# Wide matmuls in the first feed-forward product of a two-block transformer kernel

## The chip, the cores and the metric

The kernel runs on one core of one Trainium2 chip. The metric is the time of one execution on the device, in microseconds (us). Engines are named as in the profile: PE (TensorE, with its weight loads as PEld), DVE (VectorE), ACT (ScalarE), POOL (GpSimd) and SP, whose queue issues the loads of the weights.

## What is computed

Two transformer blocks over 256 tokens of width 1024, in float32. The first ends with a feed-forward part, and this is the part that the change touches:

```python
hf = rmsnorm(x, norm_ff_g[l])
z = jax.nn.relu(jnp.einsum('bsd,df->bsf', hf, w_ff1[l]))
x = x + jnp.einsum('bsf,fd->bsd', z * z, w_ff2[l])
```

Its inner width is 4096, which the kernel cuts into eight blocks of 512 columns. The second block (gated linear attention, block attention, 32 experts) follows, and its expert weights, 3 x 32 matrices of 2 MB, are the largest part of what is read.

## The kernel before

**Numbers in two parts.** Each float32 operand of a product is split into an upper part, rounded to the format fp32r, and a lower part, the remainder. A product is three matmuls: upper weights times upper activation, upper weights times lower activation, lower weights times upper activation. The weights are split on the fly: `conv` (L197 to L218) lets ACT copy a piece of 128 x 1024 into `whi` (L215), and then DVE or POOL subtracts to get `wlo` (L216). I call the ACT instruction the cast of a unit and the subtraction its split.

**Units.** Work goes in units: one unit is one such piece, half a loaded slot of 1 MB, and 24 matmuls of 256 columns. `unit_mm` (L220) records its matmuls, all in L246 for this part of the program. There are four buffers for each of `whi` and `wlo` (`NB = 4`), so the cast of unit j + 4 can only run when unit j has been multiplied, and it has the three units between them as its time. The main loop records, for unit j: the matmuls, then what evacuates a finished product, then `conv(j + 4)`, and then, while there are any, one operation of `adaq`. Splits of units with j % 4 = 1, and here also j % 8 = 4, go to POOL, three of eight; the other five go to DVE.

**The `adaq` operations** (L357) are 128 x 1024 multiply-and-sum operations on DVE that compute the second block's modulation from weights (w_adaT) loaded meanwhile. Behind every fourth there is a tiny addition (L362). 24 of them fall into the feed-forward part. They have no hurry of their own, but DVE's instructions stand in one queue, in the order written.

**The feed-forward part.** First product, block c: `f1(c)`, four units. Second product, block c: `f2(c)`, four units. The order is f1(0), f1(1), f2(0), f1(2), f2(1), f1(3), f2(2), ..., f1(7), f2(6), f2(7), which are units 80 to 143: f1(c) for c from 2 on is units 76 + 8c to 79 + 8c, f2(c) is units 88 + 8c to 91 + 8c. The result of f1(c) is used eight units later, so it is in no hurry.

**Evacuation of f1(c)** (`ev_f1`, L545 to L557), behind the last of its four units: for each of two PSUM banks, DVE takes relu and multiplies by the norm factor (L552, reading PSUM and one SBUF tile), ACT squares (L555), and `split` makes the two parts of z, the upper by ACT (L262), the lower by DVE (L264). Only then comes `conv` of unit j + 4.

Of the kernel before, what the change touches and what calls it, by code (L numbers as in the profile page):

```python
# [26 lines left out]
OV = 12  # L27

# [43 lines left out]
def tile_fused(ctx: ExitStack, tc: tile.TileContext, I, out):  # L72
# [146 lines left out]

    def unit_mm(j, units):  # L220
        g, kp = units[j]
        if g.mode == "G":
            mm_gates(convd.pop(j))
            return
        if g.mode == "L":
            if kp:
                mm_last(g, (convd.pop(j - 1), convd.pop(j)))
            return
        whi, wlo = convd.pop(j)
        ahi, alo = g.act()  # L230
        if kp == 0 and g.first:
            g.ps = [bank(b) for b in g.banks]
        if kp == 0 and not g.first:
            g.ps = g.prev.ps
        for kk in range(2):
            k = 2 * kp + kk
            ka = g.k0 + k
            lastk = g.last and k == g.nk - 1
            firstk = g.first and k == 0
            if g.mode == "F":  # L240
                for m in range(4):
                    o = g.ps[m // 2][:, (m % 2) * 256:(m % 2 + 1) * 256]
                    c = slice(m * 128, (m + 1) * 128)
                    pairs = ((whi, ahi), (whi, alo), (wlo, ahi))
                    for i, (w, a) in enumerate(pairs):
                        pe.matmul(o, w[:, kk, c], a[:, ka, :], start=firstk and i == 0 and m % 2 == 0,  # L246
                                  stop=lastk and i == 2, skip_group_check=True)
            else:
                for n in range(2):
                    o = g.ps[n]  # L250
                    c = slice(n * 128, (n + 1) * 128)
                    pairs = ((ahi, whi), (ahi, wlo), (alo, whi))
                    for i, (a, w) in enumerate(pairs):
                        pe.matmul(o, a[:, ka, c], w[:, kk, :], start=firstk and i == 0,
                                  stop=lastk and i == 2, skip_group_check=True)
        if kp == g.nk // 2 - 1 and g.last and g.evac:
            g.evac(g.ps)
# [8 lines left out]
    def half_of(name, m, t):  # L266

        return A[name][0][:, m:m + 2, :], A[name][1][:, m:m + 2, :], t
# [59 lines left out]
    A = {}  # L328
    st = {}

    def pair(tag, name):
        A[name] = tuple(big(f"{tag}{i}", (128, 8, 256), F32R) for i in range(2))
# [177 lines left out]
    def ev_wo(ch):  # L510
        def f(ps):
            if ch == 0:
                pair("E", "xg")
            for j in range(2):
                m = 4 * ch + 2 * j
                x1 = xT[:, m:m + 2, :]
                dve.tensor_tensor(x1, v2(ps[j]), x1, op=OP.add)
                for i in (m, m + 1):
                    act.activation(A["xg"][0][:, i, :], xT[:, i, :], AF.Copy, scale=V("gff", i))
            for i in range(4 * ch, 4 * ch + 4):  # L520
                dve.scalar_tensor_tensor(A["xg"][1][:, i, :], xT[:, i, :], V("gff", i),
                                         A["xg"][0][:, i, :].bitcast(F32), op0=OP.mult, op1=OP.subtract)
# [21 lines left out]
    def ev_f1(c):  # L544
        def f(ps):  # L545
            if c == 0:
                st["z"] = [big(f"H{i}", (128, 2, 4, 256), F32R) for i in range(2)]
            t4 = st["z"][c % 2]
            A["z", c] = (t4[:, 0], t4[:, 1])
# [6 lines left out]
            split(*(half_of(("z", c), 2 * j, t) for j, t in enumerate(ts)))  # L556
        return f  # L557
# [58 lines left out]
    def bn_hn():  # L616
# [34 lines left out]
    def mm_gates(w):  # L651
        ps = bank(7)
        for k in range(8):
            for i in range(2):
                pe.matmul(ps[:, 0:256], w[:, k, :], A["hn"][i][:, k, :], start=k == 0 and i == 0,
                          stop=k == 7 and i == 1)
# [109 lines left out]
    def mix_in(i, tag):  # L766
        t = big(tag, (128, 2, 4, 256), F32R)
        A["mix", i] = (t[:, 0], t[:, 1])
# [158 lines left out]
    def at_o(m, b):  # L927
# [12 lines left out]
        split((A["mix", 1][0][:, m, :], A["mix", 1][1][:, m, :], ps[:, 0:256]))  # L940
# [27 lines left out]
    def mm_last(g, w):  # L968

        ahi, alo = g.act()  # L970
        for m in (0, 2, 1, 3):
            o = g.prev.ps[m // 2][:, (m % 2) * 256:(m % 2 + 1) * 256]
            c = slice(m * 128, (m + 1) * 128)
            for k in range(4):
                whi, wlo = w[k // 2]
                for i, (x, a) in enumerate(((whi, ahi), (whi, alo), (wlo, ahi))):
                    pe.matmul(o, x[:, k % 2, c], a[:, k, :], start=False, stop=k == 3 and i == 2, skip_group_check=True)
# [193 lines left out]
    def f1(c, hooks=None):  # L1171
        add_group(next_slot(I["w_ff1"][c], 2), "F", "xg", ev_f1(c), hooks)
# [148 lines left out]
    def x_g(k):  # L1321
        hi, lo = A["xg"][0][:, k, :], A["xg"][1][:, k, :]
# [25 lines left out]
    def x_h(k0):  # L1348
        for k in range(k0, k0 + 2, 2):
            t = tmp()  # L1350
            pool.tensor_tensor(t, xT[:, k:k + 2, :], st["rxb"][:, None, :].to_broadcast([128, 2, 256]), op=OP.mult)
            for i in range(2):
                hi = A["h"][0][:, k + i, :]
                act.activation(hi, t[:, i, :], AF.Copy, scale=V("gmix", k + i))
                dve.scalar_tensor_tensor(A["h"][1][:, k + i, :], t[:, i, :], V("gmix", k + i), hi.bitcast(F32),
# [4 lines left out]
    for s in steps:  # L1360
        if s[0] == "u":
# [342 lines left out]
def layout(inputs):  # L1704
# [15 lines left out]

    a = {"x": f["x"], "xT": np.ascontiguousarray(f["x"][0].T.reshape(8, 128, 256).transpose(1, 0, 2))}
    a["w_in"] = kpc(f["w_in"][0]).reshape(7, 2, 2, 128, 2048)
    for n in ("w_proj_a", "w_proj_b", "w_out"):
        a[n] = kpc(f[n][0])
    a["w_ff1"] = kpc(f["w_ff1"][0])
# [60 lines left out]
```

## Time and profile before

| what | value |
|---|---|
| three runs, median (lowest to highest) | 1041.33 us (1040.93 to 1042.59) |
| the profiled execution's own time | 1041.49 us |
| its span, first to last instruction | 1039.8 us |
| PE busy, share of the span | 1003.6 us, 97% |
| DVE / ACT / POOL busy | 515.0 / 354.1 / 216.8 us |
| read from HBM | 325.13 MB |

Times in the trace count from the start of the span. The feed-forward part lies between about 244 and 431 us, the experts between about 600 and 1040 us. A group of instructions merged in a row has a start, a length, a count (x3) and, in brackets, the idle time of the engine just before it and what ended it. "PE busy" counts overlapping matmuls once and says little of how densely they are packed; their start times do.

### The profile page before, as it was taken

The page shows a single profiled execution, that of the slowest core. Times are in us where ns is not written, and L with a number is a line of the kernel's source. Part 1 is how long each engine was busy: PE and PEld are TensorE (multiplying, and loading weights), DVE is VectorE, ACT ScalarE, POOL GpSimd, SP SyncE. Part 2 cuts the span into 40 slices and gives each one's busy share as a digit, 9 for nine tenths or more (in the row PEclk, how much of TensorE's full clock was granted, in tenths as well). Part 3 has the DMA queues.
Part 4 walks back from the last instruction along what each step waited for, and adds up shares of the span by engine and source line. Part 5 has one row for each costly group of instructions (what it writes and reads, how often), then busy time and mean ns, then how long its engine had stood idle before and what let it go on. Part 6 is the DMA issues. An engine that isn't in the chain of part 4 may idle for free. (4 is left out here: it accounts for less than half of the span.)

```text
span 1039.8 us, 16067 instructions
## 1 busy us (share of the span) xinstructions
PE 1003.6 (97%) x6690; PEld 738.0 (71%) x6690; DVE 515.0 (50%) x767; ACT 354.1 (34%) x528; POOL 216.8 (21%) x137
## 2 busy tenths in 40 slices
PE   9999999999999999989999999999999998888996
PEld 6999999999999999878989634343434343433443
DVE  5787985477589863489784422121212121111112
ACT  6554543454543454455465311010101010100111
POOL 1333422235343334166343200000000000000100
PEclk9999999999999999999999999999999999999999
DMA  8964787665578965435649699999999999998995
GB/s 335 417 261 163 279 329 285 207 239 180 185 289 298 343 248 200 162 130 195 232 144 370 234 418 419 422 421 421 421 422 421 420 421 422 420 418 343 420 419 216
DMA packets 51796, 327.27 MB, mean 315 GB/s; under 512 B 5896, under 2 KB 8712, under 8 KB 15112
## 3 DMA queue, kind: packets, MB, share of 16 engines
q1 hardware_dynamic: 51432, 325.68, 80.4%
q8 instruction: 54, 0.88, 0.3%
q10 hardware_dynamic: 288, 0.52, 0.1%
q14 instruction: 22, 0.18, 0.0%
HBM read 325.13 MB, written 1.05 MB: 314 GB/s over the span
## 5 line engine op out<-in xcount | busy, mean ns | idle before, releaser
L215 ACT ACTIVATE whi<-w 128x1024 fp32r<-128x1024 f32 x178 | 185.6, 1057 | 175.0 <-PE P L246 149.9
L246 PE MATMUL P<-H,whi 128*128 128x256 f32 x1312 | 236.9, 283 | 0.0
L216 POOL TENSOR_TENSOR wlo<-w,whi 128x1024 fp32r<-128x1024 f32 x58 | 152.6, 2640 | 327.1 <-ACT whi L215 302.4
L216 DVE TENSOR_TENSOR wlo<-w,whi 128x1024 fp32r<-128x1024 f32 x120 | 161.2, 1355 | 105.7 <-ACT whi L215 105.7
L246 PEld LDWEIGHTS P<-H,whi 128*128 128x128 f32 x1312 | 204.6, 192 | 0.3 <-issue 0.3
L246 PE MATMUL P<-H,wlo 128*128 128x256 f32 x656 | 185.6, 283 | 0.0
L1473 PE MATMUL P<-w,whi 128*64 128x512 f32 x480 | 164.8, 602 | 3.5 <-DMA w<-in_w_up_dram 2.2
L246 PEld LDWEIGHTS P<-H,wlo 128*128 128x128 f32 x656 | 125.9, 192 | 0.0
L246 PE MATMUL P<-E,whi 128*128 128x256 f32 x672 | 121.7, 283 | 0.0
L1638 DVE SCALAR_TENSOR_TENSOR t<-t,wsl,P 128x512 f32<-128x512 f32 x16 | 12.0, 747 | 196.7 <-PE P L1473 193.4
L246 PE MATMUL P<-F,whi 128*128 128x256 f32 x576 | 106.2, 285 | 1.2 <-DVE F L627 0.8
L246 PEld LDWEIGHTS P<-E,whi 128*128 128x128 f32 x672 | 104.9, 192 | 0.1
L246 PE MATMUL P<-E,wlo 128*128 128x256 f32 x336 | 95.3, 284 | 1.3 <-DVE wlo L216 1.3
L1473 PEld LDWEIGHTS P<-w,whi 128*64 128x64 f32 x480 | 51.8, 138 | 58.9 <-issue 49.1
L246 PEld LDWEIGHTS P<-F,whi 128*128 128x128 f32 x576 | 89.9, 192 | 3.3 <-DVE F L627 1.6
L1012 POOL TENSOR_SCALAR t<-cst,prm 128x128 f32<-128x128 f32 x8 | 5.0, 640 | 392.9 <-DVE yx L264 392.9
L246 PE MATMUL P<-F,wlo 128*128 128x256 f32 x288 | 81.7, 284 | 2.6 <-DVE wlo L216 2.6
L262 ACT ACTIVATE yx<-t 128x512 fp32r<-128x512 f32 (+1 forms) x32 | 20.0, 625 | 188.1 <-DVE t L1501 188.1
L1493 PE MATMUL P<-w,t 128*64 128x512 f32 x216 | 75.2, 595 | 0.9 <-issue 0.9
L357 DVE SCALAR_TENSOR_TENSOR w<-w,M 128x1024 f32<-128x1024 f32 x44 | 73.3, 1685 | 1.5 <-DMA w<-in_w_adaT_dram 1.5
L1501 DVE TENSOR_TENSOR t<-P,yx 128x512 f32<-128x512 f32 (+1 forms) x33 | 22.3, 676 | 88.6 <-PE P L1493 88.6
L246 PEld LDWEIGHTS P<-E,wlo 128*128 128x128 f32 x336 | 64.5, 192 | 1.7 <-DVE wlo L216 1.7
(366 smaller groups left out, 1451.4 us busy)
## 6 DMA issues: line engine op xcount, KB each, us to landing
w<-in_w_in_dram SPq DMA_DIRECT2D x38, 1024.0 KB, 5.1
w<-in_w_ff_dram SPq DMA_DIRECT2D x32, 1024.0 KB, 5.0
w<-in_w_gate_dram SPq DMA_DIRECT2D x29, 1024.0 KB, 19.8
w<-in_w_down_dram SPq DMA_DIRECT2D x25, 1024.0 KB, 19.8
w<-in_w_up_dram SPq DMA_DIRECT2D x25, 1024.0 KB, 19.8
w<-in_w_adaT_dram SPq DMA_DIRECT2D x22, 1024.0 KB, 6.1
w<-in_w_out_dram SPq DMA_DIRECT2D x8, 1024.0 KB, 4.9
WL<-in_w_down_dram SPq DMA_DIRECT2D x8, 1024.0 KB, 19.3
```

The costliest lines, as they stand in the source:

```text
L215: act.activation(hi, src, AF.Copy)
L216: (pool if j % 4 == PL or j % 8 == 4 and 80 <= j < 204 or late else dve).tensor_tensor(lo, src, hi.bitcast(F32), op=OP.subtract)
L246: pe.matmul(o, w[:, kk, c], a[:, ka, :], start=firstk and i == 0 and m % 2 == 0, stop=lastk and i == 2, skip_group_check=True)
L262: act.activation(hi, src, AF.Copy)
L357: dve.scalar_tensor_tensor(w, w, 1.0, crow, op0=OP.mult, op1=OP.mult, accum_out=mod[:, 4 * i + f:4 * i + f + 1])
L1012: e.tensor_scalar(dg[:, i, :], ident, cols[:, 4 * c + i:4 * c + i + 1], None, op0=OP.mult)
L1473: pe.matmul(ps[64 * j:64 * j + 64, :], xts[i][:, k, c:c + 64], weight(p, nm, j, i, k), start=i == 0 and k == 0, stop=i == 1 and k == 3, sk ...
L1493: pe.matmul(py[64 * j:64 * j + 64, cs], hT[:, k, 64 * j:64 * j + 64], weight(p, "w_down", j, c, k)[:, cs], start=k == 0, stop=k == 3, skip ...
L1501: dve.tensor_tensor(y, py[:, cs], g2row[:, o], op=OP.mult)
L1638: dve.scalar_tensor_tensor(hs, hs, wsl[p], pu, op0=OP.mult, op1=OP.mult)
```

## The change

Blocks 2 to 7 of the first product (`WIDE = 2`) are computed in another way; blocks 0 and 1 stay.

- The two parts of an activation now lie in one tile (`Act`: 128 x 2 parts x 4 x 256, two tiles for eight k), so that one matmul can read both. The weights of blocks 2 to 7 are laid out in memory so that a slot holds 256 columns for all eight k.
- A unit is then 8 matmuls of 512 columns (upper weights times both parts, into one whole PSUM bank) and 8 of 256 columns (lower weights times the upper part, added to the bank's first half): 16 instead of 24, with the same number of columns.
- The bank holds two half sums, which have to be added. A product of two banks is finished after every second unit, and `leave` evacuates it: for each bank ACT copies the second half (L237), DVE adds the first half to it (L238); then, for both banks at once, relu and the norm factor by DVE (L597, now reading two SBUF tiles), square and upper part by ACT, lower part by DVE.
- `leave` is run behind `conv(j + 4)` of the unit, not before it. Blocks 2 to 7 take PSUM banks 0 and 1 for the first half, 2 and 3 for the second.

```diff
+    def wide_mm(g, kp, x, whi, wlo):
+        j, k0 = kp // 2, 4 * (kp % 2)
+        if k0 == 0:
+            g.ps = [bank(b) for b in g.banks[2 * j:2 * j + 2]]
+        for m, ps in enumerate(g.ps):
+            c = slice(128 * m, 128 * m + 128)
+            for k in range(k0, k0 + 4):
+                pe.matmul(v2(ps), whi[:, k - k0, c], x.parts(k), start=k == 0, stop=False, skip_group_check=True)
+                pe.matmul(ps[:, 0:256], wlo[:, k - k0, c], x.part(0, k), start=False, stop=k == 7,
+                          skip_group_check=True)
+        if k0:
+            def leave(ps=g.ps):
+                t = tmp()
+                for m in range(2):
+                    act.activation(t[:, m], ps[m][:, 256:512], AF.Copy)
+                    dve.tensor_tensor(t[:, m], ps[m][:, 0:256], t[:, m], op=OP.add)
+                g.evac(j, t)
+            st["leave"] = leave
...
+    def ev_f1w(c):
+        def f(j, t):
+            A["z", c] = Act(st["z"][c % 2])
+            dve.scalar_tensor_tensor(t, t, 0.0, st["rffb"][:, None, :].to_broadcast([128, 2, 256]),
+                                     op0=OP.max, op1=OP.mult)
+            act.activation(t, t, AF.Square)
+            split(half_of(("z", c), 2 * j, t))
...
     def f1(c, hooks=None):
-        add_group(next_slot(I["w_ff1"][c], 2), "F", "xg", ev_f1(c), hooks)
+        if c < WIDE:
+            add_group(next_slot(I["w_ff1"][c], 2), "F", "xg", ev_f1(c), hooks)
+        else:
+            group(Group(next_slot(I["w_ff1"][c], 2), "W", h_of("xg"), 0, [0, 1, 2, 3], True, True, ev_f1w(c)))
...
                 conv(j + NB, units)
+            if "leave" in st:
+                st.pop("leave")()
```

How it stands on the engines. On PE, the first matmuls of block 3 before (E_2533 is the upper, E_2534 the lower part of the activation, P a PSUM bank):

```order
L246 MATMUL P_3327<-E_2533,whi 128x256
L246 MATMUL P_3327<-E_2534,whi 128x256
L246 MATMUL P_3327<-E_2533,wlo 128x256
L246 MATMUL P_3327<-E_2533,whi 128x256
L246 MATMUL P_3327<-E_2534,whi 128x256
L246 MATMUL P_3327<-E_2533,wlo 128x256
```

And now (E_2533 holds both parts for the first four k):

```order
L230 MATMUL P_3305<-E_2533,whi 128x512
L231 MATMUL P_3305<-E_2533,wlo 128x256
L230 MATMUL P_3305<-E_2533,whi 128x512
L231 MATMUL P_3305<-E_2533,wlo 128x256
L230 MATMUL P_3305<-E_2533,whi 128x512
L231 MATMUL P_3305<-E_2533,wlo 128x256
```

Two of every three matmuls became one of twice the columns, and they alternate with the narrow ones.

On DVE, around the evacuation of block 3 before (L357 are the `adaq` operations, L216 the splits of weights):

```order
L357 SCALAR_TENSOR_TENSOR w_3200,mod<-w_3200,M 128x1024
L552 SCALAR_TENSOR_TENSOR t<-P_3327,M 128x512
L552 SCALAR_TENSOR_TENSOR t<-P_3328,M 128x512
L264 TENSOR_TENSOR H_2880<-t,H_2880 128x512 x2
L216 TENSOR_TENSOR wlo<-w_3130,whi 128x1024
L357 SCALAR_TENSOR_TENSOR w_3200,mod<-w_3200,M 128x1024
```

And now the same block (L217 is the split, L392 the `adaq` operation, L287 the lower part of z):

```order
L238 TENSOR_TENSOR t<-P_3305,t 128x256
L238 TENSOR_TENSOR t<-P_3306,t 128x256
L597 SCALAR_TENSOR_TENSOR t<-t,M 128x512
L287 TENSOR_TENSOR H_2880<-t,H_2880 128x512
L392 SCALAR_TENSOR_TENSOR w_3126,mod<-w_3126,M 128x1024
L217 TENSOR_TENSOR wlo<-w_3114,whi 128x1024
L392 SCALAR_TENSOR_TENSOR w_3169,mod<-w_3169,M 128x1024
L217 TENSOR_TENSOR wlo<-w_3114,whi 128x1024
L238 TENSOR_TENSOR t<-P_3360,t 128x256
L238 TENSOR_TENSOR t<-P_3361,t 128x256
L597 SCALAR_TENSOR_TENSOR t<-t,M 128x512
L287 TENSOR_TENSOR H_2880<-t,H_2880 128x512
```

One evacuation of four instructions became two of four, each with its own chain from DVE to ACT and back; splits and `adaq` operations keep their order among each other and stand behind them.

On ACT, around the same evacuation before (L215 are the casts of weights):

```order
L215 ACTIVATE whi<-w_3130 128x1024
L555 ACTIVATE t<-t 128x512 x2
L262 ACTIVATE H_2880<-t 128x512 x2
L215 ACTIVATE whi<-w_3130 128x1024
L215 ACTIVATE whi<-w_3203 128x1024 x2
```

And now (L216 is the cast):

```order
L237 ACTIVATE t<-P_3305 128x256
L237 ACTIVATE t<-P_3306 128x256
L599 ACTIVATE t<-t 128x512
L285 ACTIVATE H_2880<-t 128x512
L216 ACTIVATE whi<-w_3114 128x1024 x2
L237 ACTIVATE t<-P_3360 128x256
L237 ACTIVATE t<-P_3361 128x256
L599 ACTIVATE t<-t 128x512
L285 ACTIVATE H_2880<-t 128x512
L216 ACTIVATE whi<-w_3181 128x1024 x2
```

The cast of unit j + 4 now stands ahead of the evacuation, and the casts of the next two units stand behind a square (L599) that waits for DVE. The order on POOL and on SP is the same as before.

## Rows read from the trace of the kernel before

**Rows 1.** Busy time by stretch: PE, PEld, DVE, ACT, POOL, granted clock, DMA share, GB/s.

```profile
316.00:340.00 24.00, 22.65 (x187) 22.30 (x186) 22.53 (x26) 10.31 (x12) 8.27 (x3) 1.00 0.83 300
```

**Rows 2.** Instructions of PE in order of time, unit 111 of block 4: start, us.

```profile
331.34 0.28 PE L246 MATMUL P<-E,wlo 128*128 128x256 f32 x1
...
331.70 0.28 PE L246 MATMUL P<-E,wlo 128*128 128x256 f32 x1
...
335.01 0.39 PE L246 MATMUL P<-E,wlo 128*128 128x256 f32 x1 [1.35 <-DVE wlo L216]
```

**Rows 3.** Instructions of PE in order of time, first product of the kernel, 512 columns.

```profile
26.43 0.39 PE L254 MATMUL P<-wlo,F 128*128 128x512 f32 x1
...
27.11 0.39 PE L254 MATMUL P<-wlo,F 128*128 128x512 f32 x1
```

**Rows 4.** Instructions of DVE in order of time, feed-forward part.

```profile
261.96 1.29 DVE L552 SCALAR_TENSOR_TENSOR t<-P,M 128x512 f32<-128x512 f32 x2 [1.54 <-ACT M L306]
...
288.15 1.23 DVE L216 TENSOR_TENSOR wlo<-w,whi 128x1024 fp32r<-128x1024 f32 x1 [2.20 <-ACT whi L215]
...
316.20 1.28 DVE L552 SCALAR_TENSOR_TENSOR t<-P,M 128x512 f32<-128x512 f32 x2
...
331.54 3.41 DVE L216 TENSOR_TENSOR wlo<-w,whi 128x1024 fp32r<-128x1024 f32 x1
...
339.66 1.29 DVE L552 SCALAR_TENSOR_TENSOR t<-P,M 128x512 f32<-128x512 f32 x2
342.17 1.29 DVE L264 TENSOR_TENSOR H<-t,H 128x512 fp32r<-128x512 f32 x2 [1.22 <-ACT H L262]
343.64 1.23 DVE L216 TENSOR_TENSOR wlo<-w,whi 128x1024 fp32r<-128x1024 f32 x1 [0.18 <-ACT whi L215]
...
352.86 3.50 DVE L216 TENSOR_TENSOR wlo<-w,whi 128x1024 fp32r<-128x1024 f32 x3
357.87 1.93 DVE L357 SCALAR_TENSOR_TENSOR w<-w,M 128x1024 f32<-128x1024 f32 x1 [1.51 <-DMA w<-in_w_adaT_dram]
...
374.04 3.59 DVE L216 TENSOR_TENSOR wlo<-w,whi 128x1024 fp32r<-128x1024 f32 x3
```

**Rows 5.** Instructions of POOL in order of time.

```profile
261.74 2.41 POOL L216 TENSOR_TENSOR wlo<-w,whi 128x1024 fp32r<-128x1024 f32 x1 [8.22 <-ACT whi L215]
...
331.46 2.41 POOL L216 TENSOR_TENSOR wlo<-w,whi 128x1024 fp32r<-128x1024 f32 x1 [4.43 <-ACT whi L215]
...
366.97 5.84 POOL L216 TENSOR_TENSOR wlo<-w,whi 128x1024 fp32r<-128x1024 f32 x2 [8.26 <-DMA w<-in_w_ff_dram]
```

**Rows 6.** Instructions of ACT in order of time.

```profile
340.38 1.23 ACT L555 ACTIVATE t<-t 128x512 f32<-128x512 f32 x2 [5.98 <-DVE t L552]
...
357.99 1.06 ACT L215 ACTIVATE whi<-w 128x1024 fp32r<-128x1024 f32 x1 [1.75 <-PE P L246]
```

**Rows 7.** Groups by line and form: count, busy us, mean ns, idle before.

```profile
L568 DVE TENSOR_TENSOR X<-P,X 128x256 f32<-128x256 f32 x4 | 1.7, 425 | 5.3 <-PE P L977 5.3
...
L449 DVE TENSOR_TENSOR t<-t,D 128x512 f32<-128x512 f32 x4 | 2.8, 692 | 0.8 <-ACT t L446 0.8
```

**Rows 8.** Groups of ACT and DVE between 255 and 420 us.

```profile
L555 ACT ACTIVATE t<-t 128x512 f32<-128x512 f32 x16 | 9.9, 634 | 25.2 <-DVE t L552 25.0
L262 ACT ACTIVATE H<-t 128x512 fp32r<-128x512 f32 x16 | 9.1, 617 | 0.0
```

**Rows 9.** Issues of loads by SP, the first of the experts' weights.

```profile
505.16 1.17 SPq L163 DMA_DIRECT2D M<-in_w_gate_dram  x2
```

**Rows 10.** Busy time by stretch, the experts.

```profile
600.00:1040.00 440.00, 413.87 (x2088) 180.96 (x2084) 89.62 (x151) 56.22 (x108) 4.97 (x8) 0.99 0.98 403
```

**Rows 11.** The longest wait of PE in the experts, in order of time.

```profile
913.49 1.02 PE L1473 MATMUL P<-C,whi 128*64 128x512 f32 x1 [2.86 <-DVEq L1517]
```

**Rows 12.** Busy time by stretch, behind this wait.

```profile
913.50:916.90 3.40, 3.40 (x9) 1.16 (x11) 0.00 (x0) 0.00 (x0) 0.00 (x0) 0.51 1.02 419
```

More of the change, by code (lines that the diff above doesn't have):

```diff
@@ L27 @@
 OV = 12
+WIDE = 2
 PRM = {}
@@ L243, in unit_mm @@
                     c = slice(m * 128, (m + 1) * 128)
-                    pairs = ((whi, ahi), (whi, alo), (wlo, ahi))
-                    for i, (w, a) in enumerate(pairs):
-                        pe.matmul(o, w[:, kk, c], a[:, ka, :], start=firstk and i == 0 and m % 2 == 0,
+                    for i, (w, a) in enumerate(((whi, 0), (whi, 1), (wlo, 0))):
+                        pe.matmul(o, w[:, kk, c], x.part(a, ka), start=firstk and i == 0 and m % 2 == 0,
                                   stop=lastk and i == 2, skip_group_check=True)
@@ L251, in unit_mm @@
                     c = slice(n * 128, (n + 1) * 128)
-                    pairs = ((ahi, whi), (ahi, wlo), (alo, whi))
-                    for i, (a, w) in enumerate(pairs):
-                        pe.matmul(o, a[:, ka, c], w[:, kk, :], start=firstk and i == 0,
+                    for i, (a, w) in enumerate(((0, whi), (0, wlo), (1, whi))):
+                        pe.matmul(o, x.part(a, ka)[:, c], w[:, kk, :], start=firstk and i == 0,
                                   stop=lastk and i == 2, skip_group_check=True)
@@ L329, in tile_fused, with __init__, part, parts @@
     st = {}
+    class Act:
+        def __init__(self, *tiles):
+            self.tiles = tiles
+        def part(self, i, k, n=0):
+            return self.tiles[k // 4][:, i, k % 4:k % 4 + n] if n else self.tiles[k // 4][:, i, k % 4]
+        def parts(self, k):
+            return self.tiles[k // 4][:, :, k % 4]
     def pair(tag, name):
-        A[name] = tuple(big(f"{tag}{i}", (128, 8, 256), F32R) for i in range(2))
+        A[name] = Act(*(big(f"{tag}{i}", (128, 2, 4, 256), F32R) for i in range(2)))
     def h_of(n):
@@ L654, in mm_gates @@
             for i in range(2):
-                pe.matmul(ps[:, 0:256], w[:, k, :], A["hn"][i][:, k, :], start=k == 0 and i == 0,
+                pe.matmul(ps[:, 0:256], w[:, k, :], A["hn"].part(i, k), start=k == 0 and i == 0,
                           stop=k == 7 and i == 1)
@@ L968, in mm_last @@
     def mm_last(g, w):
[L970 removed]
+        x = g.act()
         for m in (0, 2, 1, 3):
@@ L1321, in x_g @@
     def x_g(k):
-        hi, lo = A["xg"][0][:, k, :], A["xg"][1][:, k, :]
+        hi, lo = (A["xg"].part(i, k) for i in range(2))
         act.activation(hi, xT[:, k, :], AF.Copy, scale=V("gmix", k))
@@ L1719, in col, with mpair, blocks @@
         return np.asarray(v).reshape(-1, 128).T
+    def mpair(w):
+        n = w.shape[1] // 512
+        return np.ascontiguousarray(w.reshape(8, 128, n, 2, 256).transpose(2, 3, 1, 0, 4)).reshape(n, 2, 128, 2048)
     a = {"x": f["x"], "xT": np.ascontiguousarray(f["x"][0].T.reshape(8, 128, 256).transpose(1, 0, 2))}
+    def blocks(w, narrow):
+        a, b = kpc(w), mpair(w)
+        for i in narrow:
+            b[i] = a[i]
+        return b
     a["w_in"] = kpc(f["w_in"][0]).reshape(7, 2, 2, 128, 2048)
@@ L1724, in layout @@
         a[n] = kpc(f[n][0])
-    a["w_ff1"] = kpc(f["w_ff1"][0])
+    a["w_ff1"] = blocks(f["w_ff1"][0], range(WIDE))
     a["w_ff2"] = rows(f["w_ff2"][0])
```

34 lines of the change are left out of this document (19 added, 15 removed).

## The prediction

> **What bounds the kernel now.** I began with busy time by stretch. In the feed-forward part PE is busy nearly all the time, but DVE is close behind: between 316 and 340 us it works 22.53 of 24.00 us, and this is a stretch in which PE is not full, 22.65 us [rows 1]. PE in order of time shows what the gap is: inside unit 111 it waits for a split, 1.35 us [rows 2], the only such wait of its matmuls in this part. So PE sets the pace here only as long as DVE delivers.
>
> Behind it everything follows in a chain. The first load of expert weights is issued at 505.16 us, when a buffer of the second block comes free [rows 9], and from 600 us to the end DMA is busy 0.98 of the time [rows 10]. What the feed-forward part loses or gains moves the start of these loads, so I carry it to the end unchanged.
>
> **What is removed: time on PE.** Matmuls of 256 columns start 0.36 us apart for three, 331.34 to 331.70, so 0.12 each [rows 2]; of 512 columns 0.68 for three, 26.43 to 27.11, so 0.227 each [rows 3]. Three narrow ones cost 0.36 us, a wide and a narrow one 0.347. A unit of eight such pairs goes from 2.88 to 2.78 us, and 24 units save 2.5 us. No row has the two kinds alternating. The bounds: nothing, if the wide ones cost what is saved; 5.1 us, if a narrow one behind a wide one starts after its columns alone (0.107 of the 0.12). I take 2.5, because each kind keeps its spacing in its own row. The Trainium skill (TensorE: Matmul & The Clock Gate, Back-to-back issue gap) gives N/2.4 + 2.5 ns, that is 109 and 216 ns, and by it the saving would be only 0.5 us; the rows lie above both figures and decide.
>
> **What is added: time in DVE's queue.** The evacuation of a block before, from its first DVE instruction at 339.66 to the next one behind it at 343.64, holds DVE for 3.98 us, of which 1.22 + 0.18 are waits for ACT [rows 4]. Now it is done twice, for half a block each. One half in a chain:
> - two additions of 256 columns from PSUM: 0.425 us for a form like it [rows 7], the second overlapping by some 0.08 us as 512-column ones do (two in 1.28), so 0.77 to the end;
> - the multiplication, 0.69 [rows 7];
> - square and copy on ACT one behind the other, 0.634 + 0.617 [rows 8], with DVE standing still;
> - the lower part, 0.61 to the next start (two in 1.29, [rows 4]);
> - four hand-overs between dependent instructions of some 0.03 us.
>
> That is 3.44 us, 6.9 for a block, 2.9 more than now. The reason is that before two tiles went through the chain together and one wait served both. The additional copies on ACT (four of 256 columns a block) lie in time in which ACT waits for PE, 1.75 us before a cast [rows 6].
>
> **A hold by POOL.** DVE's split at 331.54 took 3.41 us instead of 1.23; POOL had begun its own split 0.08 us earlier and needed 2.41 [rows 4, 5]. Both have two SBUF operands. The evacuation's multiplication at 261.96 ran beside POOL's split of 261.74 in its usual 1.29 for two: one of its operands is in PSUM. The new multiplication reads SBUF twice, so it can be held. POOL is busy 8.27 of 24 us [rows 1]; a third of the time, for 1.2 us on average, is 0.4 us each, 3.4 us for eight. As POOL may also do its split just while DVE waits for ACT, I count half, 1.7 us; the bounds are 0 and 3.4.
>
> **Whether DVE has room.** A test of the prices on the period from 316.20 to 339.66, 23.46 us [rows 4]: five splits and six adaq operations at 1.14 ((3.50 - 1.22)/2, three in a row at 352.86) are 12.5; one evacuation 4.0; three holds by POOL 7.2. The sum is 23.7, and eight units take PE 23.0. This period is full. I call loaded what lies between the first adaq operation at 283.6 and the split of unit 126, the first of the three at 374.04, which ends at about 375.3 [rows 4]. In it four evacuations stand (blocks 2 to 5), and DVE idles 2.20 and 1.51 us beside the waits counted above. So unit 126's split moves by 4 x 2.9 + 1.7 - 3.7 = 9.6 us.
>
> **What PE makes of it.** A cast follows the unit four before it, so the one at 357.99 shows that unit 118 ended at 357.8 [rows 6]; unit 126 begins seven units later, at 378.0, 2.7 us behind its split. Unit 125's split by POOL ends at 372.81 [rows 5], 2.3 us ahead of need. These distances are what PE could eat up before it waits. I let it keep them: the splits of units 124 and 125 follow casts that ACT can only make behind a square, and this square waits for DVE. It is the same as now at 340.38, where the square waited 5.98 us [rows 6], but twice a block. So PE is 9.6 us late at unit 126. What it saves up to there is lost in waiting; the last six wide units save 0.6.
>
> **The sum:** 9.6 - 0.6 = 9.0 us on the profiled execution's 1041.49, **1050.5 us**, slower by 0.9%. (That execution is 0.16 us above the median of the runs.) By the Trainium skill's gap the last six units would save 0.1 and the sum be 1051.0. Costs that I set to nothing: the four PSUM banks, since a bank is needed again eight units later; the wait of f2 for z, since four units and more lie between. The bounds of this case: at the low end no holds, the distances eaten up (2.7) and 5.1 us saved by matmuls, so 1.3 in the last six units, 9.6 - 1.7 - 2.7 - 1.3 = 3.9 us, 1045; at the high end all holds (+1.7) and additions that don't overlap (+0.6), 11.3 us, 1053.
>
> **Rivals.**
> - *PE's rate decides, faster.* Each split is wanted 8.6 us after its cast may begin (three units) and cast and split need only 2.3, so the delay might be swallowed by the four buffers. Then all 2.5 us are saved, and the time is 1039.0, or 1036.4 with 5.1. For it: in block 6 and 7 no adaq operations stand in the queue. Against: between 316 and 340 us the buffers were already used up, PE did wait [rows 1, 2], and this case needs DVE's 2.9 us a block to fit into the 1 to 2 us that are left. It decides if the longer chain costs DVE less than about 1 us a block. The Trainium skill (Perfetto Trace Analysis, Optimizing Tensor Performance) says that larger matmuls are the more efficient; the rows agree, by 4%. Chance 0.08.
> - *A draw.* POOL's splits fall into DVE's waits for ACT, eight of 1.3 us and more, so that holds get fewer by as much as the chain gets longer, and PE loses about the 2.5 us that it saves: 1041.5, within 2 us. For it: a third of DVE's period is holds now. Against: POOL's splits come when ACT has cast, and ACT is behind in the same moments. Chance 0.06.
> - *Slower still, by the clock.* Behind a wait of 2.86 us at 913.49 PE's granted clock was 0.51, which is 1.2 instead of 2.4 GHz, for 3.4 us [rows 11, 12]; behind the one of 1.35 us it stayed at 1.00 [rows 1, 2]. 10 us of waits in four blocks are 2 or 3 us a block, and if they come in one piece, each may cost another 1.7 us (half of 3.4). With three of them 1055.6. The point from which it decides is a single wait like that of 2.86 us. Chance 0.06.
>
> **The numbers.** A change of about 0.2%, 2.1 us, is about what a measurement of this kernel can tell from no change. The forecast has 0.80. Slower by more than that: 0.80 + 0.06 = 0.86. Within: 0.06. Faster: 0.08. The range that should hold 8 in 10 is that of the forecast with a part of the clock case above it, 1045 to 1055 us.
>
> **What would show it.** The matmuls alternate 0.227 and 0.12 us apart (right for the saving). DVE's block evacuations come as two stretches of about 3.4 us from the first addition, each with an idle of some 1.3 us before L287. DVE is full from 284 us to past 380, and the last adaq operation ends some 9 us later than now, at 383. PE shows about ten waits for splits, 10 to 13 us in all, most in units of blocks 3 to 6 and at splits made by POOL, and none in block 7. The first expert load is issued near 514 us. I am wrong if PE's waits in this part stay under 4 us, or if they are there and the end does not move with them.

## The result

The changed kernel takes **1050.63 us** (median of 6 runs, 1049.07 to 1051.69), the kernel before 1042.61 (6 runs beside them). The ratio is 1.008, 95% interval 1.0067 to 1.0092, or 7.0 to 9.6 us slower (8.3 by the ratio, 8.0 by the medians). The profiled execution took 1051.24 us, 9.75 more than that of before.

Lines have moved: the cast is L216 now, the split L217, the adaq operation L392, the tiny addition behind every fourth of them L397, other matmuls L270. The new ones are the wide matmul L230, the narrow one behind it L231, ACT's copy L237, the addition L238, the multiplication L597, the square L599, and z's two parts L285 and L287.

### Profile after: PE

PE in order of time (start, us), first a wide unit of block 2, then the two longest waits:

```profile
284.05 0.28 PE L231 MATMUL P<-E,wlo 128*128 128x256 f32 x1
284.16 0.40 PE L230 MATMUL P<-E,whi 128*128 128x512 f32 x1
284.39 0.28 PE L231 MATMUL P<-E,wlo 128*128 128x256 f32 x1
...
285.11 0.28 PE L231 MATMUL P<-E,wlo 128*128 128x256 f32 x1
...
330.83 0.39 PE L231 MATMUL P<-E,wlo 128*128 128x256 f32 x1 [2.62 <-POOL wlo L217]
...
357.28 0.38 PE L231 MATMUL P<-E,wlo 128*128 128x256 f32 x1 [1.83 <-POOL wlo L217]
```

From 284.05 to 285.11 are three pairs: 1.06 us, 0.353 each, with 0.11 to 0.12 from the narrow to the wide start and 0.23 to 0.24 from the wide to the narrow one. The waits are the new thing; [rows 2] had a single one of 1.35 us. The waits between 284 and 390 us, grouped (us in total, times, longest):

```profile
ACT t L599 <- DVE t L597: 33.6, 8, 7.3
...
DVE H L287 <- ACT H L285: 10.9, 8, 1.4
...
PE P L231 <- POOL wlo L217: 5.4, 6, 2.6
...
PE P L270 <- DVE wlo L217: 1.3, 2, 0.9
...
PE P L230 <- ACT whi L216: 0.2, 1, 0.2
```

PE stands still for 6.9 us in nine waits. Behind them DVE waits eight times for ACT, once a half, 1.36 us each, and ACT stands 33.6 us at eight squares until DVE has multiplied. Busy time by stretch (columns as in [rows 1]):

```profile
316.00:340.00 24.00, 20.33 (x131) 18.33 (x131) 21.14 (x28) 11.42 (x16) 7.26 (x3) 0.93 0.81 281
...
331.20:334.60 3.40, 3.40 (x13) 2.83 (x12) 3.40 (x3) 0.00 (x0) 2.95 (x1) 0.51 0.45 188
358.40:361.80 3.40, 3.40 (x12) 2.88 (x11) 3.37 (x4) 0.54 (x1) 2.13 (x1) 0.51 0.46 125
...
284.00:383.00 99.00, 92.36 (x619) 84.38 (x619) 86.11 (x102) 44.85 (x63) 33.81 (x12) 0.97 0.75 271
```

The first answers to [rows 1]: PE 20.33 in place of 22.65. Behind each of the two long waits the granted clock is 0.51, the 1.2 GHz level, for 3.4 us.

### Profile after: DVE, POOL, ACT, SP

DVE in order of time: one half's evacuation, two instructions that POOL held, the end of the loaded stretch (the last of its adaq operations is held as well).

```profile
295.27 0.75 DVE L238 TENSOR_TENSOR t<-P,t 128x256 f32<-128x256 f32 x2
296.06 0.69 DVE L597 SCALAR_TENSOR_TENSOR t<-t,M 128x512 f32<-128x512 f32 x1
298.11 0.69 DVE L287 TENSOR_TENSOR H<-t,H 128x512 fp32r<-128x512 f32 x1 [1.36 <-ACT H L285]
298.71 1.22 DVE L392 SCALAR_TENSOR_TENSOR w<-w,M 128x1024 f32<-128x1024 f32 x1
...
328.61 2.19 DVE L397 TENSOR_TENSOR mod<-mod,prm 128x4 f32<-128x4 f32 x1
...
331.86 3.38 DVE L392 SCALAR_TENSOR_TENSOR w<-w,M 128x1024 f32<-128x1024 f32 x1
...
379.66 3.42 DVE L392 SCALAR_TENSOR_TENSOR w<-w,M 128x1024 f32<-128x1024 f32 x1
...
385.29 3.48 DVE L217 TENSOR_TENSOR wlo<-w,whi 128x1024 fp32r<-128x1024 f32 x3
```

From 295.27 to 298.71 are 3.44 us for a half, where [rows 4] had 3.98 for a whole block. The last adaq operation ends at 383.08; the three splits that began at 374.04 [rows 4] begin at 385.29.

How much of DVE's time is holds can be read from its groups between the first adaq operation and these three splits (count, busy us, mean ns, idle before). Before:

```profile
L357 DVE SCALAR_TENSOR_TENSOR w<-w,M 128x1024 f32<-128x1024 f32 x24 | 44.9, 1890 | 1.5 <-DMA w<-in_w_adaT_dram 1.5
L216 DVE TENSOR_TENSOR wlo<-w,whi 128x1024 fp32r<-128x1024 f32 x18 | 23.9, 1343 | 4.6 <-ACT whi L215 4.6
...
L362 DVE TENSOR_TENSOR mod<-mod,prm 128x4 f32<-128x4 f32 x6 | 5.1, 855 | 0.2
```

And after, where no split is held:

```profile
L392 DVE SCALAR_TENSOR_TENSOR w<-w,M 128x1024 f32<-128x1024 f32 x24 | 41.9, 1762 | 0.0
...
L397 DVE TENSOR_TENSOR mod<-mod,prm 128x4 f32<-128x4 f32 x6 | 9.2, 1538 | 0.2
L597 DVE SCALAR_TENSOR_TENSOR t<-t,M 128x512 f32<-128x512 f32 x8 | 8.0, 1002 | 0.3
```

Undisturbed, these take 1.22 us (adaq operation and split), 0.16 (tiny addition) and 0.69 (multiplication). What lies above that is 22.5 us before (16.1 + 2.2 + 4.2) and 23.8 after (13.0 + 8.3 + 2.5). So POOL holds DVE for 1.3 us more than before.

POOL in order of time, at the two held instructions of 328.61 and 331.86:

```profile
327.73 6.42 POOL L217 TENSOR_TENSOR wlo<-w,whi 128x1024 fp32r<-128x1024 f32 x2 [15.36 <-ACT whi L216]
```

ACT in order of time: a cast ahead of the feed-forward part, one square with what stands behind it, two casts behind the part.

```profile
156.54 1.06 ACT L216 ACTIVATE whi<-w 128x1024 fp32r<-128x1024 f32 x1 [0.78 <-PE P L270]
...
317.40 0.63 ACT L599 ACTIVATE t<-t 128x512 f32<-128x512 f32 x1 [7.31 <-DVE t L597]
...
318.60 1.99 ACT L216 ACTIVATE whi<-w 128x1024 fp32r<-128x1024 f32 x2
...
458.99 1.99 ACT L216 ACTIVATE whi<-w 128x1024 fp32r<-128x1024 f32 x2
```

The same two casts in the kernel before:

```profile
156.03 1.06 ACT L215 ACTIVATE whi<-w 128x1024 fp32r<-128x1024 f32 x1 [0.77 <-PE P L246]
...
449.44 1.99 ACT L215 ACTIVATE whi<-w 128x1024 fp32r<-128x1024 f32 x2
```

The starts of these two casts make a ruler for the feed-forward part alone, free of the start of the program and of the experts: 293.41 us before, 302.45 after, **9.04 us more**. The first expert load (SP's issues), which answers to [rows 9], comes 10.83 us later:

```profile
515.99 0.80 SPq L164 DMA_DIRECT2D M<-in_w_gate_dram  x2
```

0.5 of that lies ahead of the first cast, and 1.3 came behind the second one, of which more below. From that load to the end of the span it is 533.5 us, before 534.6.

**Where it went.** I added up the spacing of matmul starts beyond the usual between 284 and 386 us. The nine waits cost 8.5 us, more than the 6.9 of the view, which counts a matmul's modelled end as work. The two stretches at half clock cost 3.2, from the end of the wait to the return of the full clock. The saving of the wide units takes off 1.3, the wait that stood there before 1.5. Together that is 8.9 of the ruler's 9.04.

### The profile page after: what moved, and what is told of

Same layout as the page of the kernel before. It is cut to its first block, busy times and chain, and to the rows that moved or that the text cites. A ratio compares the mean times of both kernels' runs of the same rounds, so it can differ in the third digit from the quotient of the medians.

```text
span 1049.5 us, 15738 instructions
## 1 busy us (share of the span) xinstructions
PE 1007.4 (96%) x6498; PEld 730.9 (70%) x6498; DVE 531.6 (51%) x791; ACT 360.2 (34%) x552; POOL 218.0 (21%) x137
## 5 line engine op out<-in xcount | busy, mean ns | idle before, releaser
L216 ACT ACTIVATE whi<-w 128x1024 fp32r<-128x1024 f32 x178 | 184.3, 1054 | 157.6 <-PE P L270 104.4
L270 PE MATMUL P<-H,whi 128*128 128x256 f32 x1312 | 237.0, 283 | 0.0
L217 POOL TENSOR_TENSOR wlo<-w,whi 128x1024 fp32r<-128x1024 f32 x58 | 154.1, 2663 | 335.4 <-ACT whi L216 308.1
L217 DVE TENSOR_TENSOR wlo<-w,whi 128x1024 fp32r<-128x1024 f32 x120 | 161.7, 1362 | 87.8 <-ACT whi L216 87.8
L270 PEld LDWEIGHTS P<-H,whi 128*128 128x128 f32 x1312 | 204.4, 192 | 0.6 <-issue 0.3
L270 PE MATMUL P<-H,wlo 128*128 128x256 f32 x656 | 185.8, 283 | 1.3 <-DVE wlo L217 1.3
L270 PEld LDWEIGHTS P<-H,wlo 128*128 128x128 f32 x656 | 125.8, 192 | 1.8 <-DVE wlo L217 1.8
L270 PE MATMUL P<-F,whi 128*128 128x256 f32 x576 | 107.6, 288 | 1.2 <-DVE F L671 0.8
L270 PEld LDWEIGHTS P<-F,whi 128*128 128x128 f32 x576 | 91.1, 194 | 3.3 <-DVE F L671 1.7
L270 PE MATMUL P<-F,wlo 128*128 128x256 f32 x288 | 82.4, 286 | 2.5 <-DVE wlo L217 2.5
L285 ACT ACTIVATE yx<-t 128x512 fp32r<-128x512 f32 (+1 forms) x32 | 19.9, 623 | 187.4 <-DVE t L1551 187.4
L230 PE MATMUL P<-E,whi 128*128 128x512 f32 x192 | 71.2, 411 | 0.2 <-ACT whi L216 0.2
L392 DVE SCALAR_TENSOR_TENSOR w<-w,M 128x1024 f32<-128x1024 f32 x44 | 70.3, 1615 | 0.0
L231 PE MATMUL P<-E,wlo 128*128 128x256 f32 x192 | 55.9, 291 | 5.4 <-POOL wlo L217 5.4
L270 PEld LDWEIGHTS P<-F,wlo 128*128 128x128 f32 x288 | 55.9, 194 | 3.0 <-DVE wlo L217 3.0
L270 PE MATMUL P<-E,whi 128*128 128x256 f32 x288 | 52.3, 284 | 0.0
```

The source lines that it names most:

```text
L216: act.activation(hi, src, AF.Copy)
L217: (pool if j % 4 == PL or j % 8 == 4 and 80 <= j < 204 or late else dve).tensor_tensor(lo, src, hi.bitcast(F32), op=OP.subtract)
L230: pe.matmul(v2(ps), whi[:, k - k0, c], x.parts(k), start=k == 0, stop=False, skip_group_check=True)
L231: pe.matmul(ps[:, 0:256], wlo[:, k - k0, c], x.part(0, k), start=False, stop=k == 7, skip_group_check=True)
L270: pe.matmul(o, w[:, kk, c], x.part(a, ka), start=firstk and i == 0 and m % 2 == 0, stop=lastk and i == 2, skip_group_check=True)
L285: act.activation(hi, src, AF.Copy)
```

## The experiments

The table gives for each kernel its time against the kernel before (95% interval in us, from the ratio and the median of before beside it) and the ruler, which is read from one profile each and is much finer: where nothing should change (e1) it shows 0.02 us.

| run | time against before, us | ruler against before, us |
|---|---|---|
| the change | +8.3 (7.0 to 9.6) | +9.04 |
| e1 narrow, new layout | -0.2 (-1.1 to 0.6) | -0.02 |
| e2 last two wide | -0.1 (-1.0 to 0.7) | -0.46 |
| e3 narrow, short adaq | -1.4 (-2.4 to -0.4) | -1.82 |
| e4 wide, short adaq | -3.1 (-4.3 to -2.0) | -3.10 |
| e5 wide, joint | +1.9 (1.0 to 2.8) | +1.74 |
| e6 wide, late square | -1.3 (-2.3 to -0.2) | -1.15 |
| e7 narrow, late square | -1.4 (-2.3 to -0.5) | -1.20 |
| e8 narrow, two chains | +4.8 (3.5 to 6.0) | +4.33 |
| e9 wide, splits on DVE | -0.3 (-1.4 to 0.6) | -0.55 |
| e10 wide, late square, splits on DVE | -2.8 (-3.9 to -1.9) | -3.10 |
| e11 last two wide, late square | -0.9 (-2.0 to 0.0) | -1.59 |
| e12 narrow, late square, splits on DVE | -1.3 (-2.2 to -0.3) | -1.19 |

### Is it the layout, or each wide block? (e1, e2)

e1 sets the first wide block behind the last one, e2 makes only blocks 6 and 7 wide:

```diff
-WIDE = 2
+WIDE = 8    # e1; 6 in e2
```

> The changed kernel with none of the blocks wide (the first wide block would be number 8): what is left of the change is the activations in tiles of both parts and the code around them. Theory (the loss comes from the half evacuations in DVE's queue): like the kernel before, 0.0 us, within 1.5. Rival (the tiles, or the order in which the program now stands, cost something by themselves): 3 us or more slower.

> Blocks 6 and 7 wide, 2 to 5 narrow. Behind 375 us DVE idles beside its splits, so the theory expects that the longer evacuations cost nothing there and that PE keeps its saving: eight units by 0.05 us as the changed kernel's matmuls stand, 0.4 us faster than the kernel before, which can hardly be measured; no wait of PE for a split in block 7. Rival (every wide block costs the same, 9 us / 6 = 1.5 each, wherever it stands): 3 us slower than before.

e1 is the kernel before to 0.02 us on the ruler: tiles and code order cost nothing. e2 gains 0.46 there where 0.4 was expected (its time alone, -1.0 to 0.7, can't show that), and between 284 and 440 us PE's matmuls have one wait, the old one (line, what for: total, times, longest):

```profile
PE P L270 <- DVE wlo L217: 1.4, 1, 1.4
```

So a wide block costs nothing where DVE has room. The rival of 1.5 us a block, 3 us slower, falls.

### Without DVE's load (e3, e4)

```diff
+            n = 16 if st.get("cut") else 1024
-            w = s[f // 2].tile[:, f % 2 * 1024:f % 2 * 1024 + 1024]
-            dve.scalar_tensor_tensor(w, w, 1.0, crow, op0=OP.mult, op1=OP.mult,
+            w = s[f // 2].tile[:, f % 2 * 1024:f % 2 * 1024 + n]
+            dve.scalar_tensor_tensor(w, w, 1.0, crow[:, 0:n], op0=OP.mult, op1=OP.mult,
...
-            fn(lambda: st.update(ada=True))
+            fn(lambda: st.update(ada=True, cut=True))
```

with WIDE = 8 in e3, 2 in e4.

> None of the blocks wide, and the adaq operations of the feed-forward part cut from 1024 to 16 columns each (so the sums behind the modulation are taken over a part of the row only; loads and buffers as they were). It says what DVE's load costs without the change. Theory: the one wait of PE in block 4 (1.5 us between matmul starts) goes, 1.5 us faster than the kernel before. Rival (no part of the time hangs on DVE's load): 0.0.

> The change as it is, six blocks wide, and the adaq operations of the feed-forward part cut from 1024 to 16 columns each (so the sums behind the modulation are taken over a part of the row only). Theory: with that load gone the half evacuations fit into DVE's queue, PE does not wait for splits, and its saving shows alone: 24 units by 0.05 us, 1.3 us faster than the narrow kernel with the same cut, 2.8 faster than the kernel before; the granted clock does not fall between 284 and 400 us. Rival (the wide form itself, or the chain of one half, holds PE up whatever DVE has to do): 6 to 9 us slower than the narrow kernel with the same cut.

Both come out as the theory says, and both rivals fall. e4's busy time over the whole stretch:

```profile
284.00:383.00 99.00, 99.00 (x693) 92.34 (x692) 63.81 (x110) 51.40 (x73) 31.18 (x13) 1.00 0.82 309
```

PE is full, at full clock, with the same half evacuations in DVE's queue: DVE still waits 1.36 us for ACT in each half. The difference of the two, 1.28 us on the ruler, is what the wide form is worth by itself: 0.053 for each of 24 units.

### The same wide products, evacuated in other ways (e5, e6)

e5 lets the first half wait and sends both through together. In short (the remarks behind # are mine):

```diff
-        if k0:
-            def leave(ps=g.ps):
+        if k0 and j == 0:
+            g.first_half = g.ps
+        if k0 and j:
+            def leave(pss=(g.first_half, g.ps)):
...
+                for ps, t in zip(pss, ts):
+                    for m in range(2):
+                        dve.tensor_tensor(t[:, m], ps[m][:, 0:256], t[:, m], op=OP.add)
+                    g.evac(t)       # the multiplication
+                g.evac(None, ts)    # square, copy; square, copy; both lower parts
```

> Six blocks wide as in the change, but the first half's banks wait, and both halves of a block leave together behind its last unit: all additions and multiplications on DVE first, then square and copy of one half behind the other on ACT, then both lower parts. Theory (each half pays for a wait of its own for ACT, 1.36 us): a block holds DVE for about 4 x 0.37 + 2 x 0.64 + 0.65 of waiting + 2 x 0.61 = 4.6 us in place of 6.9, so 0.6 more than the narrow one in place of 2.9; with the holds by POOL as they were, unit 126 is about 0.4 us late (4 x 0.6 + 1.7 - 3.7) and PE keeps most of its saving: within 1.5 us of the kernel before, 8 to 9 us faster than the change. Rival (the additions and the wide form cost it, the number of waits is nothing): 5 us or more slower than before.

e6 keeps the halves apart and puts the second part of each behind the next unit's cast:

```diff
-            act.activation(t, t, AF.Square)
-            split(half_of(("z", c), 2 * j, t))
+            def fin():
+                act.activation(t, t, AF.Square)
+                split(half_of(("z", c), 2 * j, t))
+            st["fin"] = fin
...
+            fin = st.pop("fin", None)
             unit_mm(j, units)
...
                 conv(j + NB, units)
+            if fin:
+                fin()
             if "leave" in st:
                 st.pop("leave")()
```

> Six blocks wide and halves that leave apart as in the change, but square, copy and lower part of a half are put behind the cast and the split of the next unit. So ACT makes a cast before it stands at the square, and DVE has a split or an adaq operation (1.14 us) between multiplication and lower part. Theory: DVE's wait of 1.36 us becomes 0.2 to 0.3, a half costs it about 2.3 in place of 3.44 us, a block 4.6, 0.6 more than the narrow one; within 1.5 us of the kernel before, 8 to 9 us faster than the change; no single wait of PE over 2 us, no fall of the granted clock between 284 and 400 us. Rival (the sum of busy time decides, not the standing still): DVE's busy time is the same as in the change, so 5 us or more slower than before.

DVE of e6 in order of time, one half from its additions to its lower part:

```profile
312.39 0.74 DVE L238 TENSOR_TENSOR t<-P,t 128x256 f32<-128x256 f32 x2
313.17 0.69 DVE L597 SCALAR_TENSOR_TENSOR t<-t,M 128x512 f32<-128x512 f32 x1
313.77 1.22 DVE L392 SCALAR_TENSOR_TENSOR w<-w,M 128x1024 f32<-128x1024 f32 x1
...
314.92 1.22 DVE L217 TENSOR_TENSOR wlo<-w,whi 128x1024 fp32r<-128x1024 f32 x1
316.06 0.69 DVE L287 TENSOR_TENSOR H<-t,H 128x512 fp32r<-128x512 f32 x1
```

The instructions are those of the change; the 1.36 us of standing still are gone, filled by an adaq operation and a split. That turns +9.04 into -1.15 us. PE has two waits left, 0.9 and 0.6 us, and the clock stays at 1.00 between 284 and 383 us. DVE is busy 94.14 of these 99 us, where it was 86.11 in the change: busy time was not what counted, the rival of e6 falls. The edit does one thing more, though: ACT makes a cast before it stands at the square, so its casts are no longer late either. e6 alone can't tell the two engines' standing apart; e9 below can.

e5, with 0.70 of waiting a block and 4.84 us in all (4.6 expected), is 1.74 us slower on the ruler and 1.9 by its time, outside the 1.5 that were expected, though far from the rival's 5; one wait of PE of 2.14 us remained, and behind it the granted clock was 0.54.

### The late square without wide products (e7), two chains without them (e8)

e7 has WIDE = 8 and the edit of e6 in the evacuation of narrow blocks:

```diff
-            for t in ts:
-                act.activation(t, t, AF.Square)
-            split(*(half_of(("z", c), 2 * j, t) for j, t in enumerate(ts)))
+            def fin():
+                for t in ts:
+                    act.activation(t, t, AF.Square)
+                split(*(half_of(("z", c), 2 * j, t) for j, t in enumerate(ts)))
+            st["fin"] = fin
```

> None of the blocks wide, and square, copy and lower part of a block put behind the cast and the split of the next unit. Theory: a block's evacuation holds DVE for about 1.2 us less, 4.8 us in the loaded part, and PE's one wait of 1.5 us goes: 1.4 us faster than the kernel before, as with the short adaq operations. Rival (that wait comes from POOL's split beside DVE's, not from the queue as a whole): 0.0.

As expected in size. The wait of block 4 went (1.8 us on the ruler with e3), and 0.6 came back elsewhere, at the first product that needs z, near 267 us, where the lower part is now late (waits of e7; 0.3 us by the view, 0.6 by the starts of the matmuls):

```profile
PE P L270 <- DVE H L287: 0.3, 1, 0.3
```

The rival said that the wait of block 4 comes from POOL's hold of one split, the one at 331.54 [rows 4]. Its forecast of 0.0 falls, but neither e3 nor e7 has a held split there, so whether the hold or the length of the queue made that wait stays open.

e8 lets a narrow block leave in two chains:

```diff
                 dve.scalar_tensor_tensor(t, v2(ps[j]), 0.0, st["rffb"][:, None, :].to_broadcast([128, 2, 256]),
                                          op0=OP.max, op1=OP.mult)
-            for t in ts:
                 act.activation(t, t, AF.Square)
-            split(*(half_of(("z", c), 2 * j, t) for j, t in enumerate(ts)))
+                split(half_of(("z", c), 2 * j, t))
```

> None of the blocks wide, but the two halves of a block's evacuation go one behind the other: multiplication, square, copy and lower part of the first half, then of the second, so that each pays for its own wait for ACT. Nothing is added or held otherwise. Theory: a half costs 0.64 + 1.36 + 0.61 = 2.6 us, a block 5.2 in place of 3.98; 4 x 1.3 - 3.7 of idle absorbed = 1.4, and so 1 to 2 us slower than the kernel before. Rival 1 (only the wide form costs): 0.0. Rival 2 (each stand of ACT at a square costs PE a wait of its own, whether DVE has room or not): 5 us or more slower.

DVE of e8 in order of time, one block's evacuation with what follows it (L586 is the narrow multiplication), and the last adaq operation:

```profile
290.94 0.69 DVE L586 SCALAR_TENSOR_TENSOR t<-P,M 128x512 f32<-128x512 f32 x1
292.99 0.69 DVE L287 TENSOR_TENSOR H<-t,H 128x512 fp32r<-128x512 f32 x1 [1.36 <-ACT H L285]
293.60 0.68 DVE L586 SCALAR_TENSOR_TENSOR t<-P,M 128x512 f32<-128x512 f32 x1
295.64 0.69 DVE L287 TENSOR_TENSOR H<-t,H 128x512 fp32r<-128x512 f32 x1 [1.36 <-ACT H L285]
296.59 1.23 DVE L217 TENSOR_TENSOR wlo<-w,whi 128x1024 fp32r<-128x1024 f32 x1 [0.26 <-ACT whi L216]
...
377.56 3.41 DVE L392 SCALAR_TENSOR_TENSOR w<-w,M 128x1024 f32<-128x1024 f32 x1
```

The size was missed: 4.3 to 4.8 us where 1 to 2 were expected. A block takes 5.65 us, 1.67 more than 3.98, so 6.7 for four. Held instructions of DVE last 24.0 us beyond their usual time where it was 22.5, 1.5 more. Of the 3.7 us of idle time only the 1.51 were absorbed: the 2.20 at 288.15 [rows 4] stand ahead of the first of the four evacuations. Together 6.7, and the last adaq operation does end at 381.0 in place of 373.9, 6.7 us later when the start's 0.4 are taken off. PE lost 4.33 of that; here it did eat up its distances. What stands: two waits in place of one, with nothing wide and nothing added, cost half of what the change costs.

The 5 us of rival 2 lie within the interval (3.5 to 6.0), and the first of PE's five waits is of its kind, as this cast stood behind both squares of a block:

```profile
324.04 0.50 PE L270 MATMUL P<-H,whi 128*128 128x256 f32 x2 [1.44 <-ACT whi L216]
```

So e8 by itself can't set ACT's standing aside. Against rival 2 is e4, where each half makes ACT stand and PE is full all the same, and e9, further below.

### Splits from POOL to DVE (e9, e10, e11, e12)

```diff
-            (pool if j % 4 == PL or j % 8 == 4 and 80 <= j < 204 or late else dve).tensor_tensor(...)
+            (pool if not 96 <= j < 132 and (j % 4 == PL or j % 8 == 4 and 80 <= j < 204 or late) else dve).tensor_tensor(...)
```

e9 has this alone, e10 with e6's edit. e11 is e6's and e7's edit with WIDE = 6, and e12 is e7 with the splits on DVE.

> The change as it is, but the twelve weight splits that POOL makes between about 285 and 383 us (units 96 to 131) are made by DVE. Theory with the hold as a cost (a POOL split takes 2.4 us and holds DVE's instruction with two SBUF operands beside it by about as much): in the profile of the change eleven of DVE's instructions are held there, 21.7 us in all; these go, and twelve splits of 1.14 us, 13.7, come. DVE's queue gets 8 us shorter, unit 126 is 1 to 2 us late in place of 9.3: 7 to 8 us faster than the change, within 2.5 us of the kernel before. Rival (the holds lie in time that nobody needs, only the count of DVE's own work matters): 13.7 us more in a full queue, 10 us or more slower than the change.

> Six blocks wide, square, copy and lower part of a half behind the next unit's cast and split, and the splits of units 96 to 131 on DVE. Theory: what the late square and the splits give DVE back add up, PE does not wait for splits, and the saving of the wide products shows whole, as with the short adaq operations: 3 us faster than the kernel before. Rival (the late square has used up what there was to get): 1.2 us faster, as with the late square alone.

Busy time of e9 over the stretch, and behind its longest wait of PE (1.69 us):

```profile
284.00:383.00 99.00, 96.95 (x671) 89.72 (x670) 84.52 (x122) 48.26 (x68) 0.00 (x0) 1.00 0.82 300
...
328.50:332.00 3.50, 3.50 (x20) 3.09 (x21) 3.50 (x6) 1.23 (x2) 0.00 (x0) 1.00 0.86 300
```

POOL is empty, DVE makes 34 splits in these 99 us in place of 17 and is busy 84.52 us in place of 86.11. No instruction of DVE in the stretch is held. The loss of 9.04 us is gone, 9.6 us gained on the ruler where 7 to 8 were expected; the expectation had left out a hold of 2.1 us behind the last adaq operation, with which it is 23.8 in all. And DVE still waits 1.36 us in each half, and ACT stands at the squares as long as in the change (waits of e9 between 284 and 390 us; 33.6 us at eight in the change):

```profile
ACT t L599 <- DVE t L597: 32.6, 9, 5.0
```

So ACT's standing costs nothing by itself. Nor is it POOL's own pace: e6 leaves the splits on POOL, and there the loss is gone too. What counts is how late DVE is with its queue; the delay reaches PE by way of ACT, whose casts stand behind the square, and of POOL, which splits behind the cast. e10's row:

```profile
284.00:383.00 99.00, 99.00 (x692) 92.24 (x691) 86.46 (x125) 53.00 (x73) 0.00 (x0) 1.00 0.83 311
```

PE is full. It is 2.8 us faster than the kernel before, and on the ruler exactly what the short adaq operations gave, with the whole work done. This is the fastest complete version of the study.

> Blocks 6 and 7 wide, 2 to 5 narrow, square, copy and lower part of every evacuation behind the next unit's cast and split. Theory: the gain of the late square in the narrow blocks (1.4 us) and the saving of the last eight wide units (0.45 us between the casts of the earlier run) add up: 1.8 us faster than the kernel before, and no wait of PE for a split. Rival (with wide and narrow blocks mixed a new wait comes): 1 us or less faster.

> The best kernel so far without its wide products: none of the blocks wide, square, copy and lower part behind the next unit's cast and split, the splits of units 96 to 131 on DVE. It says what of the 3 us is the wide form's. Theory: without waits of PE the narrow kernel gains what it gained with the short adaq operations, 1.8 us between the casts, and the wide form 24 x 0.053 = 1.3 us beyond that: 1.4 to 1.8 us faster than the kernel before. Rival (the relief of DVE is all of the gain): 2.8 us faster, as with the wide products.

e11 adds up on the ruler: -1.20 of e7 and -0.46 of e2 are -1.66, measured -1.59; its time alone could not tell that from the rival. e12 stands within 0.01 us of e7 on the ruler, a little short of the 1.4 to 1.8 us that were expected: with no wait of PE left in the loaded stretch more relief gives nothing, and its rival (2.8 us) falls. Of e10's 3.1 us the wide products are thus 1.9 against e12, of which 0.6 are e12's own late z; the clean figure is the 1.28 of e3 and e4.

## Why the prediction was right

**The forecast's course.** The sum was 9.0; the ruler shows 9.04. The last adaq operation was to end at 383, it ended at 383.08. The chain of one half was to take 3.44 us, it took 3.44, with DVE standing 1.36. The cause, DVE's queue, is shown by e4 (the load taken away: nothing lost), e9 (only the holds taken away, with twelve splits added: the loss gone) and e6 (only the standing still taken away, DVE's and ACT's); e8 (only the standing still added) shows that a chain for each half costs by itself.

**That it met 9.04 so closely is partly luck.** Unit 126's split was to move by 9.6 us. It moved from 374.04 to 385.29, 10.8 us later counted from the first adaq operation. In the trace the longer chain gave 11.7 of it (11.6 forecast), the holds 1.3 (1.7), and idle time absorbed 3.5 (3.7). A term that was set at nothing, DVE's wait for ACT's copies, gave 1.3. On the other side PE was to keep its distance of 2.7 us and ate up 1.4 of it, so that it came to unit 126 9.4 us late. The two errors, 1.2 and 1.4, cancel.

**Terms that were mis-sized.**
- *What PE saves.* The step "three narrow ones cost 0.36 us, a wide and a narrow one 0.347" failed by half: the wide start is followed at 0.23 to 0.24, not 0.227, a pair takes 0.353 us, and 24 units save 1.3 (e4 against e3), not 2.5. The rule of the Trainium skill (TensorE: Matmul & The Clock Gate, Back-to-back issue gap), by which it would have been 0.5, was too low as well. It hardly moved the sum, as the forecast lets PE's saving drown in waits but for the last six units, 0.3 instead of 0.6.
- *The hold by POOL*, counted 1.7 between 0 and 3.4. Two of the eight multiplications were held, by 1.25 each, 2.5 in all; the other holds fell by 1.2, so the sum of all of them rose by 1.3, from 22.5 to 23.8. Right within its bounds, but I saw it only as an addition to the new multiplication. That the old holds of 22.5 us are the larger store, and cost more than POOL's twelve splits save, could have been read from [rows 4, 5], and I did not draw the conclusion; e9 does. The Trainium skill (SBUF — State Buffer, Who interferes with whom) says that a DVE instruction with two SBUF inputs contends with a GpSimd one that reads SBUF, and that the port pair they share is an exclusive lock. The trace agrees: an addition of 128x4, 0.16 us elsewhere, took 2.19 beside POOL's split.
- *PE's waits.* About ten, 10 to 13 us, were announced; nine came, 6.9 us by the view and 8.5 by the starts, six at POOL's splits, none in block 7. The two stretches at half clock, which the sum did not have, made 3.2 more.

**The rivals.** *PE's rate decides* fell by the waits, *a draw* too: POOL's splits held DVE for 1.3 us more, not less. *Slower still, by the clock*: the mechanism came, two falls of 3.4 us, but behind waits of 2.62 and 1.83 us, below the 2.86 that I had set, and the time did not rise to 1055.6. My reading is that PE only arrived later at waits it had to make anyway, since DVE set the pace: in the stretch DVE waited for PE's results only once behind the falls, 0.56 us before 365.82. No run separates the falls from the waits, so this is argued, not shown.

**What lies between 9.0 and the end.** The profiled execution was 9.75 us longer than that of before. Behind the second cast another fall of the clock cost 1.3 us (460 to 464.5 us, 0.62); the two waits of PE ahead of it, 0.85 and 0.92 us, are those of the kernel before, 0.83 and 0.94, where the clock stayed at 1.00. The fall is also in e8, e10 and e12, where the next cast comes 6.43 us later in place of 4.94, and it is missing in the other runs, e6 and e7 among them. So it goes with none of these edits alone; on what it does hang stays open. The start shifted by 0.5 and the experts gave back 1.1: 9.04 + 1.3 + 0.5 - 1.1 is the 9.75.

## What to carry to other kernels

Before a block's work is cut into halves, count the waits in the chain of its evacuation: two tiles that go through together share one wait, two that go apart pay for two, and in a full queue the standing still costs as much as work. The cure is order: put the next unit's work between the two ends of a hand-over to another engine, so that neither engine stands in front of the other. And look at what a helper engine's instruction does to its neighbour before it is given work: here twelve splits on POOL saved DVE 13.7 us (12 x 1.14) and held it for 23.8.

## What the hardware showed that I had not expected

The granted clock fell behind single waits of PE that were shorter than the one I knew. Waits in the wide units and the granted clock right behind them: 1.69 us, 1.00 (e9); 1.83, 0.51 and 2.62, 0.51 (the change); 2.14, 0.54 (e5, the row below). The length of one wait does not decide it alone: behind the 0.85 and 0.92 us of the change the clock fell too, and behind 0.83 and 0.94 in the kernel before it did not.

```profile
329.30:332.70 3.40, 3.40 (x12) 2.89 (x12) 3.40 (x3) 0.00 (x0) 3.12 (x1) 0.54 0.50 210
```

And POOL's split is itself longer beside DVE's long instructions: two in 6.42 us, 3.2 each, where [rows 5] had 2.41 for one and 5.84 for two. With the adaq operations short (e4) all of POOL's splits between 284 and 383 us took 2.41 on average:

```profile
L217 POOL TENSOR_TENSOR wlo<-w,whi 128x1024 fp32r<-128x1024 f32 x13 | 31.2, 2412 | 70.9 <-ACT whi L216 61.8 <-DMA w<-in_w_ff_dram 9.1
```
